# Both S5 runs in the projection phase, seven PSUM slots for the first projection, and the last gate by halves, in a hybrid trunk step

## The chip, the cores and the metric

The kernel runs on one core of a Trainium2 chip. The metric is the time of one execution on the device in microseconds; the median of three runs stands for the kernel. The engines have the names of the profile: PE multiplies matrices, PEld loads their stationary operand, DVE, ACT and POOL work on elements, and SP issues the DMA transfers.

## The reference

One layer of a streaming encoder works on 2080 tokens: 2048 of a prompt and 32 of a second group with states of its own. All projections have 1024 rows; `w_in` is worked as 22 tiles of 128 columns and eight more for beta and alpha; the hidden layer has 2816 columns.

```python
hn   = rmsnorm(h, norm_mix)
proj = hn @ w_in                                   # qkv | z | beta,alpha | u5 | cc
ya = gdn_mixer(qkv, z, ba, ...)                    # conv of 4, chunked delta rule, state per head
yb = s5_mixer(u5, ...)                             # diagonal complex scan over time, GLU
yc = conformer_conv(cc, ...)                       # GLU, causal conv of 31 taps, LayerNorm, swish
h  = h + concat([ya, yb, yc]) @ w_out
hf = rmsnorm(h, norm_ffn)
h  = h + (silu(hf @ w1) * (hf @ w3)) @ w2
h  = h + (p @ pe_w) * sigmoid(h @ pe_gate_w)
y  = rmsnorm(h, norm_final)
```

The results are y and the new states of the three mixers, all in float32. The delta rule and the S5 scan pass a state from one stretch of tokens to the next; the conformer reads 30 earlier columns.

## The kernel before

Activations lie with features on partitions and tokens as columns. The tokens are cut into four blocks: three of 512 columns, and a last of 544, which is worked through in two chunks of 272 since a PSUM slot holds 512. Each float32 product is made of three passes, high x high, high x low and low x high, where high is the rounded part of an operand and low the rest. `dense` issues the 3 x 8 matmuls of one output tile into a PSUM slot. `load_weight` loads a weight tile (128 x 1024, 512 KB) into one of three buffers, ACT makes its high part (L94) and, the first time, POOL the low part (L98; DVE for w3); the low part is kept in memory and only loaded afterwards (L93).

Phase A (`PhaseA.block`) normalises a block's input, makes its halves hh and hl, and projects it tile by tile; DVE or ACT evacuates each tile (qkv: raw at L615; the conformer's input: xc at L723), and results go to memory. Phase F (`PhaseF.block`) takes a block from w_out to the output: it loads the heads' result mixT into hb and splits it into fah and fal (`split`, L77, L1134 to L1136), multiplies by w_out (evacuation L1173, square sums L1163 to L1167), normalises, runs hidden tiles (L1196 to L1204) and w2 (L1218), splits hb once more, and for each of eight tiles m runs the pe and gate products (L1241 to L1243). Then come the sum of squares over all columns and the final norm: `rms_bcast` makes the factor for each column, hb is multiplied by it (three tiles on POOL, L1251, five on DVE, L1253), and stored (L1254).

The three mixers, called heads, are Python generators ("chains"). A chain is a sequence of steps; each yield ends one, and a yield of k waits for k turns. `dense` calls `G.step`, which advances every chain once per `G.stage` columns of dense matmuls (7168, in phase F's first block 9216), so that heads are written in between dense tiles. `G.flush(done)` advances the chains until done. The head work of one block is `conf_of(b)`, whose convolution is 62 DVE instructions with the name cacc (L824, L826), and `gdn_of(b)`, two groups of 256 tokens and, in the last block, one of 32. S5 runs twice, `s5_unit` u = 0 and 1, each for two blocks (`G.UB` = 2).

Before the change the first S5 run, beside conformer 0 and gdn 0, is advanced in phase A. All other heads are one chain, `later_heads`, in phase F: conformer 1, gdn 1, conformer 2, S5 run 1, gdn 2, conformer 3, gdn 3. Block b of phase F starts only once heads b are done (`G.flush`). In the order that results, the convolution of conformer 1 has been pulled into phase A's last block.

Within an engine, instructions run in the order in which they are written out after the Tile scheduler has placed them: the code gives each a priority class (`G.first`, `G.heads`, `G.later`), and the scheduler's own timeline picks among those that are ready. PSUM has eight banks: three slots pd (`G.psD`) for dense tiles, one pn for norms, and two each of pc and pm (`G.psM`) for heads. SP's queue holds nearly all transfers in one order.

Of the kernel before, what the change touches and what calls it, by code (L numbers as in the profile page):

```python
# [2 lines left out]

# [5 lines left out]
F32 = mybir.dt.float32  # L9
# [414 lines left out]
def s5_unit(G, A, u, wp, pspool):  # L424
# [14 lines left out]
    for jq in range(4):  # L439
# [15 lines left out]
        Gm = ld("G", [P, 2, 2, P], G.s5c["G"][:, js])  # L455
        Toep = ld("Toep", [P, 4, P], G.s5c["Toep"][:, jq * 4:jq * 4 + 4])

        yield 3

        w = [wp.tile([P, 2, NCT], F32, tag=f"w{i}", name=f"w{i}") for i in range(2)]  # L460
        tm = [wp.tile([P, 2, NCT], F32, tag=f"tm{i}", name=f"tm{i}") for i in range(4)]
# [50 lines left out]
                else:  # L512
                    V.tensor_copy(S1[half[h], js, i], X[h][half[i], :, NC])

        yield 4

        ys = wp.tile([P, 4, NCT], F32, tag="ys", name="ys")
        ysv = ys.rearrange("p (j h) c -> p j h c", h=2)
# [25 lines left out]
        nc.scalar.activation(t, t, AF.Tanh, scale=math.sqrt(2.0 / math.pi))  # L544
        nc.scalar.activation(yf, yf, AF.Copy, scale=0.25)
        V.scalar_tensor_tensor(gq[:, jh], t, 1.0, yf, op0=ALU.add, op1=ALU.mult)
        yield 1 if jh == 0 else 5
    spc = 512 // NCT
    for j in range(2):
        yb = wp.tile([P, n], F32, tag="yf", name="yb")  # L550
# [21 lines left out]
class PhaseA:  # L572


    def __init__(self, G, A, ctx):
        self.G, self.A = G, A
        nc = G.nc
        V = nc.vector
        E = lambda name, bufs=1, **k: ctx.enter_context(G.tc.tile_pool(name=name, bufs=bufs, side="left", reuse_waits="tile", **k))
        self.wp = E("aw", 2)  # L580
        self.xp = E("ax", 12)
        cp = E("ac")

# [49 lines left out]
    def block(self, b):  # L633
# [481 lines left out]
class PhaseF:  # L1115
# [22 lines left out]
    def block(self, b):  # L1138
# [19 lines left out]
            hb.append(h)  # L1158
        ssum = wp.tile([P, n], F32, tag="ssum", name="ssum2", bufs=1)

        def squares(m):
            if m == 0:
                nc.scalar.activation(ssum, hb[m], AF.Square)  # L1163
            else:
                sq = wp.tile([P, n], F32, tag="t0", name="sq2")
                nc.scalar.activation(sq, hb[m], AF.Square)
                V.tensor_tensor(ssum, ssum, sq, op=ALU.add)  # L1167

        for m in range(KD):
            w = load_weight(G, A.w_out[m], KD, "out", m)  # L1170
# [57 lines left out]
            self.split(x, y, mx, k % 2)  # L1228
            ph.append((x, y))
        ssum = wp.tile([P, n], F32, tag="ssum", name="ssum3", bufs=1)  # L1230
        for m in range(KD):
            if m % 4 == 0:
                wp4 = load_weight(G, A.pe_w[m:m + 4].rearrange("m p k c -> p m k c"), (4, 2), "pe", m)
            wpe = [x[:, m % 4] for x in wp4]
            wg = load_weight(G, A.pe_gate[m], KD, "gate", m)
            for c0, cn in ch:
                cs = slice(c0, c0 + cn)
                pe = dense(G, G.psD, "pd", wpe, lambda k: ph[k][0], lambda k: ph[k][1], [0, 1], c0, cn)
                pg = dense(G, G.psD, "pd", wg, lambda k: ah[k], lambda k: al[k], ks, c0, cn)
                th = wp.tile([P, 512], F32, tag="t1", name="gth2")[:, :cn]  # L1240
                nc.scalar.activation(th, pg[:, :cn], AF.Tanh, scale=0.5)  # L1241
                V.scalar_tensor_tensor(th, th, 1.0, pe[:, :cn], op0=ALU.add, op1=ALU.mult)
                V.scalar_tensor_tensor(hb[m][:, cs], th, 0.5, hb[m][:, cs], op0=ALU.mult, op1=ALU.add)  # L1243
            squares(m)
            if m < 3:
                nc.scalar.activation(hb[m], hb[m], AF.Copy, scale=self.g3[:, m:m + 1])
        bc = wp.tile([P, n], F32, tag="bc", name="bc3", bufs=1)
        rms_bcast(G, wp, G.psN, "pn", ssum, n, bc)
        for k in range(KD):
            if k < 3:  # L1250
                nc.gpsimd.tensor_tensor(hb[k], hb[k], bc, op=ALU.mult)  # L1251
            else:
                V.scalar_tensor_tensor(hb[k], hb[k], self.g3[:, k:k + 1], bc, op0=ALU.mult, op1=ALU.mult)  # L1253
            nc.sync.dma_start(A.yT[:, k, t0:t0 + n], hb[k])  # L1254


@with_exitstack
def trunk_kernel(ctx: ExitStack, tc: tile.TileContext, A):
# [8 lines left out]
    def at(which):  # L1267
# [121 lines left out]
    def conf_of(b):  # L1389
        with R(f"cc_{b}") as wp:  # L1390
            yield from conf(b, wp)

    def s5_of(u):
        with R(f"s5_{u}") as wp:
            yield from s5_unit(G, A, u, wp, G.psM)

    def gdn_of(b):
        with R(f"gd_{b}", 2) as sp:
            for i in range(2):
                state[0] = yield from gdn_part(b, i, state[0], sp)  # L1400

    def run(*gens):

        for g in gens:
            yield from g

    with ExitStack() as cx:
        pa = PhaseA(G, A, cx)
        pa.block(0)

        box = {}

        def first_s5():
            while "w5" not in box:
                yield 1
            yield from s5_unit(G, A, 0, box["w5"], G.psM)
            box["done"] = True

        def first_heads():
            with R("s5i") as tp:  # L1420
                yield from s5_init(G, A, tp, G.psM)
            with R("s5_0") as w5:
                box["w5"] = w5
                yield from conf_of(0)
                yield from gdn_of(0)
                while "done" not in box:
                    yield 1

        G.start(first_heads())
        for b in range(1, NB):  # L1430
            if b == G.UB:
                G.start(first_s5())
            pa.block(b)
        if NB == G.UB:
            G.start(first_s5())
        G.flush()
    pf = PhaseF(G, A, ctx)
    ready = [0]

    def later_heads():  # L1440
        for b in range(1, NB):
            yield from conf_of(b)
            if b % G.UB == 0:
                yield from s5_of(b // G.UB)
            yield from gdn_of(b)
            ready[0] = b

    G.start(later_heads())
    for b in range(NB):
        G.flush(lambda: ready[0] >= b)  # L1450
        G.stage = STAGE.get(b, STAGE["A"])
        pf.block(b)

# [114 lines left out]
```

## Time and profile before

| | |
|---|---|
| median of three runs | 2884.57 us (2880.83 to 2887.48) |
| the profiled execution | 2888.11 us, its span 2886.3 us |
| mean granted clock | 0.979 |
| bytes moved by DMA | 565.32 MB |
| ACT, POOL busy | 935.2 us (32%), 549.4 us (19%) |

The profile shows one execution. Its rows are of three kinds: the page (busy time of each engine, a strip of 40 slices), tables by stretch of time, and single instructions with what they waited for. A name such as `ps_d<-fah,wh_gate` reads output from inputs; ps_d is a dense tile, fah and fal are the halves of an activation, wh and wl those of a weight. The share of busy time is a mean over the stages, so that a stage with an idle PE is looked for by its stretch.

### The profile page before, as it was taken

How to read it: one execution, taken by the hardware profiler on the slowest of the kernel's cores; microseconds unless marked ns; L12 is line 12 of the kernel's file. 1: busy time of each engine (PE TensorE's matmuls, PEld its weight loads, DVE VectorE, ACT ScalarE, POOL GpSimd, SP SyncE). 2: the span in 40 equal slices, each digit the busy share in tenths (PEclk: the TensorE clock that was granted, in tenths of full speed). 3: DMA queues.
4: the chain of work that ended last, by engine and by line, in shares of the span. 5: the costliest groups of instructions: out<-in, count | busy, mean ns of one | idle time of the engine just before them, and what ended most of it. 6: DMA issues, size and time to landing. Idle time of an engine off the chain costs nothing.

```text
span 2886.3 us, 41015 instructions
## 1 busy us (share of the span) xinstructions
PE 2763.9 (96%) x15300; PEld 2359.9 (82%) x15300; DVE 1751.6 (61%) x3933; ACT 935.2 (32%) x1409; POOL 549.4 (19%) x460
## 2 busy tenths in 40 slices
PE   7899999999999999899999999999999979999997
PEld 5668778898878887688888887778888869999997
DVE  8969765865675847966563755856464733333343
ACT  4243423313422222343422333342332423222232
POOL 5731312234232323421010101000010110000000
PEclk9999999999999999999999999999999979999998
DMA  6578777657654555487665657566565654555553
GB/s 225 170 252 269 248 227 227 199 181 245 206 185 167 190 168 200 152 288 220 216 183 176 187 174 242 187 207 192 172 193 154 197 193 149 174 175 176 175 187 107
DMA packets 278919, 565.32 MB, mean 196 GB/s; under 512 B 67344, under 2 KB 126880, under 8 KB 278576
## 3 DMA queue, kind: packets, MB, share of 16 engines
q1 hardware_dynamic: 278720, 562.70, 60.4%
q8 instruction: 121, 1.98, 0.3%
q14 instruction: 78, 0.64, 0.1%
HBM read 457.76 MB, written 104.25 MB: 195 GB/s over the span
## 4 chain that ended last, share of the span: by engine, by line
PE 64%; DVE 8%; DMA 3%; issue 3%; SPq 1%; ACT 1%; POOL 0%; DVEq 0%; POOLq 0%; ACTq 0%
PE ps_d L122 57%; DVE cacc L826 3%; PE ps_kk L935 1%; PE ps_q L1013 1%; PE ps_z L1026 1%; DVE ct L982 1%; DVE cx L983 1%; DVE hb L1218 1%; DMA xd<-cx 1%; DMA hb<-mixT 1%; PE ps_vn L1069 0%; PE ps_o L1083 0%; PE ps_o L1084 0%; PE ps_s L1076 0%; PE ps_ks L1056 0%
## 5 line engine op out<-in xcount | busy, mean ns | idle before, releaser
L94 ACT ACTIVATE wh_w<-wr_w 128x1024 fp32r<-128x1024 f32 (+1 forms) x272 | 281.3, 1034 | 762.9 <-PE ps_d L122 551.4
L122 PE MATMUL ps_d<-fah,wh_w 128*128 128x512 f32 (+1 forms) x1760 | 379.4, 354 | 7.4 <-DVE fa L1196 2.9
L122 PE MATMUL ps_d<-fal,wh_w 128*128 128x512 f32 (+1 forms) x1760 | 376.5, 353 | 0.0
L122 PE MATMUL ps_d<-fah,wl_w 128*128 128x512 f32 (+1 forms) x1760 | 376.1, 353 | 0.0
L122 PEld LDWEIGHTS ps_d<-fah,wh_w 128*128 128x128 f32 x1760 | 291.1, 189 | 53.6 <-issue 4.0
L122 PEld LDWEIGHTS ps_d<-fal,wh_w 128*128 128x128 f32 x1760 | 291.4, 189 | 43.2
L122 PEld LDWEIGHTS ps_d<-fah,wl_w 128*128 128x128 f32 x1760 | 291.3, 189 | 43.2 <-issue 0.4
L1218 DVE TENSOR_TENSOR hb<-hb,ps_d 128x512 f32<-128x512 f32 (+1 forms) x240 | 139.7, 583 | 167.1 <-PE ps_d L122 166.7
L122 PE MATMUL ps_d<-acth,wh_w 128*128 128x512 f32 (+1 forms) x880 | 210.3, 355 | 9.1 <-DVE hb L1218 7.7
L122 PE MATMUL ps_d<-acth,wl_w 128*128 128x512 f32 (+1 forms) x880 | 210.1, 354 | 0.0
L122 PE MATMUL ps_d<-actl,wh_w 128*128 128x512 f32 (+1 forms) x880 | 208.6, 354 | 0.0
L826 DVE SCALAR_TENSOR_TENSOR cacc<-xc,cc_w,cacc 128x512 f32<-128x512 f32 (+1 forms) x240 | 189.4, 824 | 0.0
L122 PEld LDWEIGHTS ps_d<-acth,wh_w 128*128 128x128 f32 x880 | 148.6, 189 | 34.7 <-DVE hb L1218 6.1
L122 PEld LDWEIGHTS ps_d<-actl,wh_w 128*128 128x128 f32 x880 | 149.4, 189 | 22.2
L122 PEld LDWEIGHTS ps_d<-acth,wl_w 128*128 128x128 f32 x880 | 149.2, 189 | 22.2
L98 POOL TENSOR_TENSOR wl_w<-wr_w,wh_w 128x1024 fp32r<-128x1024 f32 (+1 forms) x46 | 108.2, 2351 | 253.9 <-ACT wh_w L94 226.3
L1201 DVE SCALAR_TENSOR_TENSOR fth<-ps_d,bc 128x512 f32<-128x512 f32 (+1 forms) x110 | 64.8, 589 | 132.0 <-PE ps_d L122 131.3
L1196 DVE TENSOR_TENSOR fa<-ps_d,bc 128x512 f32<-128x512 f32 (+1 forms) x110 | 64.5, 588 | 118.5 <-PE ps_d L122 109.4
L122 PE MATMUL ps_d<-hh,wh_qkv 128*128 128x512 f32 (+1 forms) x480 | 107.2, 365 | 13.8 <-DVE raw L615 13.0
L1204 DVE TENSOR_TENSOR actl<-fa,acth 128x512 fp32r<-128x512 f32 (+1 forms) x110 | 81.3, 739 | 51.3 <-ACT acth L1203 50.9
L1199 DVE SCALAR_TENSOR_TENSOR fa<-fth,fa 128x512 f32<-128x512 f32 (+1 forms) x110 | 73.1, 667 | 58.8 <-ACT fth L1198 58.6
L122 PE MATMUL ps_d<-hh,wl_qkv 128*128 128x512 f32 (+1 forms) x480 | 105.5, 361 | 2.3 <-POOL wl_qkv L98 2.3
(479 smaller groups left out, 4783.3 us busy)
## 6 DMA issues: line engine op xcount, KB each, us to landing
wr_w<-in_w SPq DMA_DIRECT2D x256, 512.0 KB, 4.3
wl_w<-lo_w SPq DMA_DIRECT2D x192, 512.0 KB, 4.0
lo_w<-wl_w SPq DMA_DIRECT2D x64, 512.0 KB, 2.9
wr_qkv<-in_w_in SPq DMA_DIRECT2D x48, 512.0 KB, 4.7
wl_qkv<-lo_qkv SPq DMA_DIRECT2D x36, 512.0 KB, 4.2
wr_out<-in_w_out SPq DMA_DIRECT2D x32, 512.0 KB, 5.2
wr_gate<-in_pe_gate SPq DMA_DIRECT2D x32, 512.0 KB, 4.3
wl_out<-lo_out SPq DMA_DIRECT2D x24, 512.0 KB, 5.9
```

The source lines that it names most:

```text
L94: nc.scalar.activation(wh, wr, AF.Copy)
L98: e.tensor_tensor(wl, wr, wh.bitcast(F32), op=ALU.subtract)
L122: nc.tensor.matmul(ps[:, :cn], a[:, i, :], x(k)[:, c0:c0 + cn], start=start and p_ == 0 and i == 0, stop=stop and p_ == 2 and i == K - 1)
L826: V.scalar_tensor_tensor(acc[:, j], xc[:, j, t:t + W], cn_.w[:, j, t:t + 1], acc[:, j], op0=ALU.mult, op1=ALU.add)
L935: nc.tensor.matmul(kk4[:, h - h0], kq[:, 2 * h, cw], kq[:, 2 * h:2 * h + 2, cw], start=True, stop=True)
L982: V.tensor_tensor(t, cx[:, 0:nq, j:j + 1].to_broadcast(sh), cu[:, j:j + 1, j + 1:].to_broadcast(sh), op=ALU.mult)
L983: V.tensor_tensor(cx[:, 0:nq, j + 1:], cx[:, 0:nq, j + 1:], t, op=ALU.subtract)
L1196: V.tensor_tensor(a, p1[:, :cn], bc[:, cs], op=ALU.mult)
L1199: V.scalar_tensor_tensor(a, th, 1.0, a, op0=ALU.add, op1=ALU.mult)
L1201: V.scalar_tensor_tensor(th, p3[:, :cn], 0.5, bc[:, cs], op0=ALU.mult, op1=ALU.mult)
L1204: V.tensor_tensor(fb[:, cs], a, fa[:, cs].bitcast(F32), op=ALU.subtract)
L1218: V.tensor_tensor(hb[m][:, c0:c0 + cn], hb[m][:, c0:c0 + cn], p_[:, :cn], op=ALU.add)
```

## The change

Three things are changed. First, both S5 runs are one chain of their own, `s5_chain`, started in phase A ahead of the third block; run u waits until the projections of its blocks have been written (`G.u5`). Its three long yields are shortened by one turn each. The other heads are `heads_chain`, in which conformer 1 follows as soon as both S5 runs are done; phase A's flush stops once heads 0 are done. One of twelve input buffers of phase A (pool "ax") goes. Second, in block 0's projection the dense tiles take turns on seven PSUM slots instead of three. Third, in the last block the pe and gate products, the square sums, the final norm and the stores are run for the first 272 columns, then for the second; the weights are loaded twice for it. In the second half all eight final products are on DVE, and the pre-scaling on ACT is left out.

```diff
 def dense(...):
     if ps is None:
+        pool, tag = next(G.banks) if G.banks else (pool, tag)
         ps = pool.tile([P, 512], F32, tag=tag, name="ps_d")
 # s5_unit
-        yield 3
+        yield 2
...
-        yield 4
+        yield 3
...
-        yield 1 if jh == 0 else 5
+        yield 1 if jh == 0 else 4
 # PhaseA
-        self.xp = E("ax", 12)
+        self.xp = E("ax", 11)
...
+        G.u5 = b + 1
 # PhaseF.block
-        for m in range(KD):
...
-            for c0, cn in ch:
...
-            squares(m)
-            if m < 3:
-                nc.scalar.activation(hb[m], hb[m], AF.Copy, scale=self.g3[:, m:m + 1])
-        rms_bcast(G, wp, G.psN, "pn", ssum, n, bc)
...
+        for grp in ([[c] for c in ch] if len(ch) > 1 else [ch]):
+            gs = slice(grp[0][0], grp[-1][0] + grp[-1][1])
+            end = b == G.NB - 1 and gs.stop == n
+            for m in range(KD):
+                if m % 4 == 0:
+                    wp4 = load_weight(G, A.pe_w[m:m + 4]..., (4, 2), "pe", m)
+                wg = load_weight(G, A.pe_gate[m], KD, "gate", m)
+                for c0, cn in grp:
...
+                squares(m, gs)
+                if m < 3 and not end:
+                    nc.scalar.activation(hb[m][:, gs], hb[m][:, gs], AF.Copy, scale=self.g3[:, m:m + 1])
+            rms_bcast(G, wp, G.psN, "pn", ssum[:, gs], gs.stop - gs.start, bc[:, gs])
+            for k in range(KD):
+                if k < 3 and not end:
+                    nc.gpsimd.tensor_tensor(hb[k][:, gs], hb[k][:, gs], bc[:, gs], op=ALU.mult)
+                else:
+                    V.scalar_tensor_tensor(hb[k][:, gs], hb[k][:, gs], self.g3[:, k:k + 1], bc[:, gs], op0=ALU.mult, op1=ALU.mult)
+                nc.sync.dma_start(A.yT[:, k, t0 + gs.start:t0 + gs.stop], hb[k][:, gs])
 # trunk_kernel
+    def s5_chain():
+        while "w5" not in box:
+            yield 1
+        for u in range(G.NU):
+            while G.u5 < (u + 1) * G.UB:
+                yield 1
+            yield from s5_unit(G, A, u, box["w5"], G.psM)
+            box["runs"] = u + 1
+    def ready(b):
+        return box["ready"] >= b and box["runs"] * G.UB > b
+    def heads_chain():
+        with R("s5i") as tp:
+            yield from s5_init(G, A, tp, G.psM)
+        with R("s5_0") as w5:
+            box["w5"] = w5
+            yield from conf_of(0)
+            yield from gdn_of(0)
+            box["ready"] = 0
+            while box["runs"] < G.NU:
+                yield 1
+        for b in range(1, NB):
+            yield from conf_of(b)
+            yield from gdn_of(b)
+            box["ready"] = b
...
+        G.banks = cycle([(G.psD, "pd"), (G.psM, "pc"), (G.psD, "pd"), (G.psM, "pm"), (G.psD, "pd"), (G.psM, "pc"), (G.psM, "pm")])
         pa.block(0)
+        G.banks = None
+        G.start(heads_chain())
         for b in range(1, NB):
-            if b == G.UB:
-                G.start(first_s5())
+            if b == min(G.UB, NB - 1):
+                G.start(s5_chain())
             pa.block(b)
-        G.flush()
+        G.flush(lambda: ready(0))
...
-    def later_heads():
-        for b in range(1, NB):
-            yield from conf_of(b)
-            if b % G.UB == 0:
-                yield from s5_of(b // G.UB)
-            yield from gdn_of(b)
-            ready[0] = b
```

The order of the instructions shows the effect at three places. On PE, at the passage from the third to the last block of phase F, before: the gate's last pass, then the last group of the delta rule (ps_vn to ps_ot) with the final norm of the third block (ps_ss, ps_bc) among it, then w_out.

```order
L122 MATMUL ps_d<-fal,wh_gate 128x512 x8
L1069 MATMUL ps_vn<-rk,X 32x128 x4
L151 MATMUL ps_ss<-ones,ssum_20261 128x1 x4
L1076 MATMUL ps_s<-vn,rk 128x128 x4
L1083 MATMUL ps_o<-Sd_18742,kq 32x128
L1084 MATMUL ps_o<-vn,AQ 32x128
```

```order
L134 MATMUL ps_bc<-ident,rso 128x128 x4
L1109 MATMUL ps_ot<-ident,o 128x32 x4
L122 MATMUL ps_d<-fah,wh_out 128x272 x22
```

Now, at the same place:

```order
L125 MATMUL ps_d<-fah,wh_gate 128x512 x8
L125 MATMUL ps_d<-fah,wl_gate 128x512 x8
L125 MATMUL ps_d<-fal,wh_gate 128x512 x8
L125 MATMUL ps_d<-fah,wh_out 128x272 x8
L125 MATMUL ps_d<-fah,wl_out 128x272 x8
L125 MATMUL ps_d<-fal,wh_out 128x272 x5
```

The last group of the delta rule has moved up; its last ps_ot stands 227 dense matmuls ahead of the third block's end.

SP's queue at that passage, before: the last group's transfers (xd, X, zy), the third block's stores, then mixT and its loads into hb.

```order
L991 DMA X<-xd 32x4x32
L88 DMA wr_out<-in_w_out 128x1024
L1105 DMA zy<-zgd_70 128x4x32
L1384 DMA out_gdn_s<-S 128x512
L1254 DMA out_yT<-hb 128x512 x8
L1111 DMA mixT_62<-zy 128x4x32
L1155 DMA hb<-mixT_62 128x544 x8
```

Now the loads of hb stand among the third block's gate weights:

```order
L89 DMA wr_pe<-in_pe_w 128x4x256
L1115 DMA mixT_62<-zy 128x4x32
L1159 DMA hb<-mixT_62 128x544 x3
L94 DMA wl_gate<-lo_gate2_11547 128x1024
L1159 DMA hb<-mixT_62 128x544 x5
L89 DMA wr_gate<-in_pe_gate 128x1024
```

They have moved ahead of the gate's last low parts (tiles 3 to 7) and of the stores.

On DVE, in the first block's w_out, before: evacuations of w_out (L1173) and square sums (L1167) alone.

```order
L1167 TENSOR_TENSOR ssum_6921<-ssum_6921,sq_7051 128x512
L1173 TENSOR_TENSOR hb<-hb,ps_d 128x512
L1167 TENSOR_TENSOR ssum_6921<-ssum_6921,sq_7092 128x512
L1173 TENSOR_TENSOR hb<-hb,ps_d 128x512
L1167 TENSOR_TENSOR ssum_6921<-ssum_6921,sq_7133 128x512
```

Now three or six steps of conformer 1's convolution stand between two evacuations:

```order
L1177 TENSOR_TENSOR hb<-hb,ps_d 128x512
L830 SCALAR_TENSOR_TENSOR cacc<-xc,cc_w,cacc 128x512 x3
L1171 TENSOR_TENSOR ssum_7449<-ssum_7449,sq_7625 128x512
L830 SCALAR_TENSOR_TENSOR cacc<-xc,cc_w,cacc 128x512 x3
L1177 TENSOR_TENSOR hb<-hb,ps_d 128x512
```

That convolution has moved here from the projection phase. On SP, in the last block's gate, the first half's stores now stand in the queue ahead of the second half's last weights:

```order
L89 DMA wr_gate_26299<-in_pe_gate 128x1024
L1262 DMA out_yT<-hb_20699 128x272
L1262 DMA out_yT<-hb_20684 128x272
```

```order
L1262 DMA out_yT<-hb_20719 128x272
L94 DMA wl_gate_26257<-lo_gate5_11754 128x1024
L94 DMA wl_gate_26302<-lo_gate6_11820 128x1024
L89 DMA wr_gate_26344<-in_pe_gate 128x1024
L94 DMA wl_gate_26347<-lo_gate7_11886 128x1024
```

Eight stores have moved in ahead of three low parts and one weight.

More of the change, by code (lines that the diff above doesn't have):

```diff
@@ L2 @@
 from contextlib import ExitStack, contextmanager
+from itertools import cycle
 import concourse.bass as bass
@@ L1159, in block, with squares @@
         ssum = wp.tile([P, n], F32, tag="ssum", name="ssum2", bufs=1)
-        def squares(m):
+        def squares(m, cs=slice(0, n)):
             if m == 0:
-                nc.scalar.activation(ssum, hb[m], AF.Square)
+                nc.scalar.activation(ssum[:, cs], hb[m][:, cs], AF.Square)
             else:
-                sq = wp.tile([P, n], F32, tag="t0", name="sq2")
-                nc.scalar.activation(sq, hb[m], AF.Square)
-                V.tensor_tensor(ssum, ssum, sq, op=ALU.add)
+                sq = wp.tile([P, n], F32, tag="t0", name="sq2")[:, cs]
+                nc.scalar.activation(sq, hb[m][:, cs], AF.Square)
+                V.tensor_tensor(ssum[:, cs], ssum[:, cs], sq, op=ALU.add)
         for m in range(KD):
@@ L1230, in block @@
         ssum = wp.tile([P, n], F32, tag="ssum", name="ssum3", bufs=1)
-        for m in range(KD):
[L1232 to L1235, printed above, removed]
-            for c0, cn in ch:
[L1237 to L1243, printed above, removed]
-            squares(m)
-            if m < 3:
-                nc.scalar.activation(hb[m], hb[m], AF.Copy, scale=self.g3[:, m:m + 1])
@@ L1247, in block @@
-        bc = wp.tile([P, n], F32, tag="bc", name="bc3", bufs=1)
-        rms_bcast(G, wp, G.psN, "pn", ssum, n, bc)
[L1249 to L1254, printed above, removed]
+        bc = wp.tile([P, n], F32, tag="bc", name="bc3", bufs=1)
+        for grp in ([[c] for c in ch] if len(ch) > 1 else [ch]):
[3 more added lines that the diff above has]
+                if m % 4 == 0:
+                    wp4 = load_weight(G, A.pe_w[m:m + 4].rearrange("m p k c -> p m k c"), (4, 2), "pe", m)
+                wpe = [x[:, m % 4] for x in wp4]
+                wg = load_weight(G, A.pe_gate[m], KD, "gate", m)
+                for c0, cn in grp:
+                    cs = slice(c0, c0 + cn)
+                    pe = dense(G, G.psD, "pd", wpe, lambda k: ph[k][0], lambda k: ph[k][1], [0, 1], c0, cn)
+                    pg = dense(G, G.psD, "pd", wg, lambda k: ah[k], lambda k: al[k], ks, c0, cn)
+                    th = wp.tile([P, 512], F32, tag="t1", name="gth2")[:, :cn]
+                    nc.scalar.activation(th, pg[:, :cn], AF.Tanh, scale=0.5)
+                    V.scalar_tensor_tensor(th, th, 1.0, pe[:, :cn], op0=ALU.add, op1=ALU.mult)
+                    V.scalar_tensor_tensor(hb[m][:, cs], th, 0.5, hb[m][:, cs], op0=ALU.mult, op1=ALU.add)
+                squares(m, gs)
[8 more added lines that the diff above has]
+                nc.sync.dma_start(A.yT[:, k, t0 + gs.start:t0 + gs.stop], hb[k][:, gs])
@@ L1277, in at @@
             tc.cur_priority = G.pr[old]
+    G.banks = None
     G.chains = []
+    G.u5 = 0
     G.acc = 0
@@ L1391, in conf_of @@
             yield from conf(b, wp)
-    def s5_of(u):
-        with R(f"s5_{u}") as wp:
-            yield from s5_unit(G, A, u, wp, G.psM)
     def gdn_of(b):
@@ L1405, in run @@
             yield from g
+    box = {"ready": -1, "runs": 0}
+    def s5_chain():
[22 more added lines that the diff above has]
+            box["ready"] = b
@@ L1407, in trunk_kernel @@
     with ExitStack() as cx:
         pa = PhaseA(G, A, cx)
+        G.banks = cycle([(G.psD, "pd"), (G.psM, "pc"), (G.psD, "pd"), (G.psM, "pm"), (G.psD, "pd"), (G.psM, "pc"), (G.psM, "pm")])
         pa.block(0)
[L1411 to L1427, printed above, removed]
@@ L1429, in trunk_kernel @@
-        G.start(first_heads())
+        G.banks = None
+        G.start(heads_chain())
         for b in range(1, NB):
-            if b == G.UB:
-                G.start(first_s5())
+            if b == min(G.UB, NB - 1):
+                G.start(s5_chain())
             pa.block(b)
-        if NB == G.UB:
-            G.start(first_s5())
-        G.flush()
+        if NB == 1:
+            G.start(s5_chain())
+        G.flush(lambda: ready(0))
     pf = PhaseF(G, A, ctx)
-    ready = [0]
-    def later_heads():
-        for b in range(1, NB):
-            yield from conf_of(b)
-            if b % G.UB == 0:
-                yield from s5_of(b // G.UB)
-            yield from gdn_of(b)
-            ready[0] = b
@@ L1448, in trunk_kernel @@
-    G.start(later_heads())
     for b in range(NB):
-        G.flush(lambda: ready[0] >= b)
+        G.flush(lambda: ready(b))
         G.stage = STAGE.get(b, STAGE["A"])
```

## The prediction

> **What bounds the kernel now.** I read the page's totals and slices first, then the stretches in which TensorE idles, the list of TensorE's waits, and the timeline at those places. In the page the first row gives busy time, share of the span and instructions of each engine; the others give busy tenths in 40 slices of 72 us, PEclk the granted clock.
>
> ```profile
> PE 2763.9 (96%) x15300; PEld 2359.9 (82%) x15300; DVE 1751.6 (61%) x3933; ACT 935.2 (32%) x1409; POOL 549.4 (19%) x460
> PE   7899999999999999899999999999999979999997
> DVE  8969765865675847966563755856464733333343
> PEclk9999999999999999999999999999999979999998
> ```
>
> PE is busy 96% of 2886.3 us, and the change takes no dense matmul away; only waits and lowered clock can be won. They sit in the first slices, slice 17, slice 33 and at the end. The windows below (from:to, length, busy us and instructions of PE, PEld, DVE, ACT, POOL, then clock, DMA share, GB/s) cover block 0's projection, the first w_out, two conformer stretches, the start of the last block, its hidden layer, and the tail.
>
> ```profile
> 62.00:155.00 93.00, 77.35 (x312) 61.69 (x310) 92.27 (x214) 25.85 (x37) 66.47 (x78) 0.91 0.54 178
> 706.00:772.00 66.00, 65.28 (x299) 53.38 (x298) 38.98 (x45) 27.19 (x37) 18.80 (x9) 1.00 0.66 225
> 1128.00:1212.00 84.00, 68.83 (x269) 51.66 (x268) 83.13 (x99) 25.15 (x37) 34.91 (x17) 0.94 0.45 156
> 1789.00:1860.00 71.00, 65.35 (x284) 52.66 (x284) 69.56 (x103) 23.98 (x32) 6.23 (x5) 0.98 0.65 224
> 2315.00:2360.00 45.00, 24.55 (x120) 18.78 (x119) 18.67 (x34) 10.59 (x16) 10.63 (x8) 0.62 0.55 189
> 2420.00:2805.00 385.00, 385.00 (x3072) 385.00 (x3072) 138.08 (x312) 105.68 (x161) 5.35 (x4) 1.00 0.54 175
> 2866.00:2886.30 20.30, 2.81 (x15) 2.09 (x15) 9.15 (x12) 1.76 (x4) 6.04 (x4) 0.60 0.29 110
> ```
>
> PE loses 15.7, 15.2, 5.7, 20.4 and 17.5 us in rows 1, 3, 4, 5 and 7, and more by the clock; the second row, the first w_out, loses 0.7, and the hidden layer nothing: there a matmul of 272 columns takes 385/3072 = 0.125. The waits (total, times, longest, us) name who was late:
>
> ```profile
> PE ps_d L122 <- DVE raw L615: 15.0, 7, 5.8
> PE ps_d L122 <- ACT fah L1134: 10.6, 7, 5.7
> PE ps_ot L1109 <- DVE o L1101: 10.1, 1, 10.1
> PE ps_d L122 <- DVE xc L723: 5.3, 1, 5.3
> PE ps_v L468 <- DMA c_PT<-s5PTre: 2.4, 1, 2.4
> PE ps_v L468 <- DMA c_PT<-s5PTim: 1.8, 1, 1.8
> ```
>
> **1. Start of the last block's w_out: −26.** S5's second run moves ahead, so heads 2 and 3 finish earlier; in the order the last head matmul now stands 227 dense matmuls (52 us at 0.23, by the rows behind) before the end of the preceding block. Timeline rows (start, us, instruction, idle before):
>
> ```profile
> 2313.52 2.00 PE L122 MATMUL ps_d<-fal,wh_gate 128*128 128x512 f32 x8
> 2319.97 1.47 PE L1069 MATMUL ps_vn<-rk,X 32*32 32x128 f32 x8 [4.45 <-DMA X<-xd]
> 2340.88 0.63 PE L1109 MATMUL ps_ot<-ident,o 32*128 32x32 f32 x4 [10.10 <-DVE o L1101]
> 2347.25 6.77 PE L122 MATMUL ps_d<-fah,wh_out 128*128 128x272 f32 x22 [5.74 <-ACT fah L1134]
> ```
>
> From the last gate matmul's end (2315.5) to the first w_out matmul 31.7 us pass, and 22 matmuls then take 6.77 instead of 2.76 (22 x 0.125): 35.7 lost. What stays: the head's and the norm's matmuls (24.55 busy in 2315:2360, of which 12.75 are w_out's from 2347.25 on: 11.8 at half clock, 6 at full); and some 3.5 for w_out's input, whose eight halves ACT makes after the gate has let go of the buffers. 35.7 − 9.5 = 26. Bounds: −30 if the halves come without delay (35.7 − 6), −20 if the head's matmuls keep their 11.8 in their new place. At the boundary before, ACT waits for the loads too:
>
> ```profile
> 1778.63 0.63 ACT L1134 ACTIVATE fah<-hb 128x512 fp32r<-128x512 f32 x1 [4.91 <-DMA hb<-mixT]
> 1772.32 2.00 PE L122 MATMUL ps_d<-fah,wl_gate 128*128 128x512 f32 x8
> 1774.16 2.00 PE L122 MATMUL ps_d<-fal,wh_gate 128*128 128x512 f32 x8
> 1779.32 0.50 PE L122 MATMUL ps_d<-fah,wh_out 128*128 128x512 f32 x1 [3.16 <-ACT fah L1134]
> 1780.59 6.11 PE L122 MATMUL ps_d<-fah,wh_out 128*128 128x512 f32 x17 [0.78 <-ACT fah L1134]
> ```
>
> Eight matmuls of 512 columns go in 1.84 (1772.32 to 1774.16), 0.23 each. This boundary loses 3.2 + 0.8 + 2.2 (6.11 against 17 x 0.23) = 6.1. Its last head now ends 352 matmuls, 81 us, earlier; the wait for the loads goes and that for the halves, 3.5, is late next: **−3** (0 to −6).
>
> **2. The conformers: +6.** Without S5 between them, the 62 DVE accumulations of conformer 1 move from the projection into the first w_out, those of 2 from the end of the first block's gate over the whole of it, those of 3 from the third block's w_out to the second block's hidden layer and gate.
>
> ```profile
> 225.00:294.00 69.00, 0.17 (x2) 0.28 (x2) 43.93 (x62) 1.00 0.78 252
> 1128.00:1212.00 84.00, 0.76 (x4) 0.56 (x4) 59.25 (x62) 0.94 0.45 156
> 1177.71 3.20 DVE L826 SCALAR_TENSOR_TENSOR cacc<-xc,cc_w,cacc 128x512 f32<-128x512 f32 x2
> 1173.14 4.05 DVE L826 SCALAR_TENSOR_TENSOR cacc<-xc,cc_w,cacc 128x512 f32<-128x512 f32 x6
> 1177.31 2.39 POOL L98 TENSOR_TENSOR wl_gate<-wr_gate,wh_gate 128x1024 fp32r<-128x1024 f32 x1 [9.04 <-ACT wh_gate L94]
> ```
>
> The first two rows are windows for the accumulations alone: 62 take 43.9 in the projection, 59.25 where POOL subtracts weights. Two beside a 2.39 us subtraction took 3.20, six without one 4.05: 1.9 is lost per subtraction. By the order, conformer 1 now runs from the third w_out tile to the sixth hidden tile, some 57 us of PE. DVE needs 43.9, then 15 for eight subtractions (706:772 has 9 POOL instructions in 66 us), then 20 of evacuations and sums (83.13 − 59.25 = 23.9 in 84 us of 1128:1212): 79 against 57. The excess is 22; six of it PE's three slots can cover, so **+16** (0 to 23), nearest to 1128:1212, where PE lost 15.2 in the same company. Conformer 2 cost 15.2 and 4 to 5 of clock there and now spreads over eight tiles, still beside subtractions: **−5** (−13 to +8). Conformer 3 cost 5.7 and 1.4 in 1789:1860; where it goes POOL rarely subtracts: **−5** (−7 to 0).
>
> Skill against row: the Trainium skill, "SBUF — State Buffer", section "SBUF: two separate sides", says the port pair of DVE and GpSimd is an exclusive lock, the loser blocked for the other's whole instruction. The 1.9 agrees nearly; with the full 2.39, eight subtractions would cost 19, not 15, and this term be +20. It speaks against the change.
>
> ```profile
> 1201.01 3.36 PE L122 MATMUL ps_d<-fah,wh_gate 128*128 128x512 f32 x7 [2.97 <-ACT gth L1241]
> 1200.00:1205.00 5.00, 3.99 (x11) 3.21 (x12) 5.00 (x5) 1.90 (x3) 2.55 (x1) 0.66 0.26 93
> ```
>
> Seven matmuls take 3.36 instead of 1.61 after 2.97 us of idleness, clock 0.66: such a stall costs 1.7 more than its length. The six covered microseconds may be eaten by this, which the upper bound holds. The Trainium skill, "TensorE: Matmul & The Clock Gate", section "HAM oscillation", puts the danger at gaps over about 3.4 us; this row's gap is shorter, the measurement decides.
>
> **3. S5's second run in the projection: +4.** It adds no PE work; its tables are loaded before it, and PE waited 2.4 + 1.8 for them in the first run. Those 4.2 I take again (0 to 9, twice that; no gain, since in the old place it showed no wait of its own). What DVE does for it lies beside dense work that has DVE to spare (38.98 of 66 in 706:772).
>
> **4. Seven slots in block 0: −9.** PE waited 15.0 for raw (evacuations of qkv) and 5.3 for xc: 20.3, with a clock of 0.91 beside it. More slots let PE run ahead, but DVE is busy 92.27 of 93 in 62:155 and its order hardly changes, so a wait returns when DVE's queue sets the end. Between 0 and −22 I take −9, nearer to zero because DVE is full.
>
> **5. Pool "ax" 12 to 11: +1.5.** One tile fewer for the projection's input; it hits the prefetch of the next block only. Nearest is one late split or load, 0 to 2.8.
>
> **6. Gate and norm of the last block by halves: +1.**
>
> ```profile
> 2868.91 1.25 PE L151 MATMUL ps_ss<-ones,ssum 128*128 128x1 f32 x10 [3.03 <-DVE ssum L1167]
> 2874.87 6.88 DVE L1253 SCALAR_TENSOR_TENSOR hb<-hb,g,bc 128x544 f32<-128x544 f32 x5 [2.66 <-ACT bc L139]
> 2866.34 0.44 DVE L1242 SCALAR_TENSOR_TENSOR gth<-gth,ps_d 128x272 f32<-128x272 f32 x1 [2.88 <-ACT gth L1241]
> 2805.00:2866.00 61.00, 60.39 (x479) 59.93 (x477) 19.32 (x39) 21.25 (x35) 0.12 (x1) 1.00 0.37 123
> 1240.00:1260.00 20.00, 20.00 (x105) 16.30 (x104) 12.42 (x24) 5.96 (x8) 5.71 (x4) 1.00 0.91 324
> ```
>
> Tail: the final scaling falls from 6.88 to eight at 0.44 (3.5): −3.4; squares, sums and broadcast over 272 columns, by halving their share, −1.8; shorter last store −0.5: −5.7. Against it: the first half's norm puts its own small matmuls on PE, 1.6, and its sum stands in the order between the second half's matmuls, so that a wait for ssum delays the gate behind it, 1.7 (3.03 in the row less what is queued ahead). Loads: 8 gate and 2 pe weights twice, high and low, are 20 more of 512 KB, 10.5 MB, and SP's queue has eight stores ahead of three of them. The 61 us of the gate moved 7.5 MB at 123 GB/s; with 10.5 and about 1.1 of stores it is 19.1 in 61 us, 313 GB/s. The row reaches 324 over 20 us, so it just fits: +3.5 (0, to 13 at the 259 of the next row).
>
> ```profile
> 165.00:345.00 180.00, 174.05 (x799) 134.53 (x799) 137.26 (x256) 77.16 (x117) 40.06 (x49) 0.97 0.80 259
> ```
>
> −5.7 + 1.6 + 1.7 + 3.5 = +1.
>
> **Sum:** −26 − 3 + 6 + 4 − 9 + 1.5 + 1 = −25.5. The profiled execution took 2888.1, so 2862.6 there; it stands 3.5 (0.12%) above the median 2884.57, which gives **2859**.
>
> **Rivals.**
> - *Slots idle.* DVE sets block 0's pace as before, and S5's loads cost double: −25.5 + 9 + 5, 2873. For it: 92.27 of 93. Against: waits of 5.8 at a time come in bursts, and bursts are what slots absorb.
> - *Conformer 1 hidden.* PE's slots and DVE's slack take it, as in the projection at 225, which lost next to nothing: −16 more, 2843. Against: POOL's subtractions.
> - *Slower: convolution exposed.* If DVE, being in order, puts the accumulations ahead of what w_out needs (19 in a row stand before the first hidden tile), PE idles for all of conformer 1: 59 instead of 16, 2902. It decides once conformer 1 costs 47 or more. For: DVE's 83.13 of 84 at 1128. Against: the order otherwise puts 3 to 6 between evacuations.
> - *Weights late in the halves.* At 259 GB/s 19.1 MB take 74 us, not 61: 9.5 over my 3.5, 2869. Slower than before would need 205 GB/s.
> - *The boundary stays.* The heads are early, but a load of mixT or the weights behind it come late through SP's one queue, and w_out still waits as long: 2859 + 26, 2885, no change. Against: the loads now stand among the gate's weights, ahead of those of its last tiles.
>
> **How the numbers follow.** A change under 0.2% (5.8 us) can't be told from none here. Forecast, 2850 to 2868: 0.47. Slots idle 0.15. Conformer hidden 0.15. Late weights 0.09. Boundary stays 0.05. Convolution exposed 0.06. The other 0.03 is divided over all signs: faster 0.87, same 0.06, slower 0.07. The range 2840 to 2880 takes in the first four cases, 0.86, and leaves out the rest and the outer spread of those, about 0.2.
>
> **What would show it.** After the last gate matmul of the third block, w_out within 6 us at full clock and no row o L1101 ahead of it; the w_out window of the first block with DVE full and PE losing about 16; the waits for raw about halved; a tail near 15 us; waits for wh_gate or wl_gate in the second half if loads are late. The prediction is wrong if conformer 1 costs nothing or over 40, or if the wait at the boundary only changes its name.

## The result: slower, and the profile after

The changed kernel takes 2911.15 us (median of four, 2908.99 to 2915.45) against 2885.98 in the same series: ratio 1.0092, 95% interval 1.0074 to 1.0111. Forecast was 2859, faster. The profiled execution took 2908.99 us, its span 2907.2, so 20.9 more than the span before.

The page after, same rows as those shown of before:

```profile
PE 2765.9 (95%) x15303; PEld 2357.5 (81%) x15303; DVE 1761.0 (61%) x3952; ACT 944.0 (32%) x1429; POOL 540.6 (19%) x461
```

```profile
PE   8789799999999999989999999999999999999997
DVE  8967874655887576697637449763745543333343
PEclk9899999999999999999999999999999999999999
```

PE's busy time is the same within 2 us; 18.9 us more of idleness make the difference. The dip at slice 33 is gone, and slices 2, 3 and 5 have become worse. A table by stages places it. First before, then after: the projection, then the four blocks of phase F, each from its first w_out matmul (from:to, length, PE busy, and so on; the third number from the end is the clock).

```profile
0.00:683.00 683.00, 634.55 (x3487) 528.59 (x3488) 508.78 (x1291) 226.55 (x359) 231.35 (x267) 0.97 0.69 220
683.00:1231.00 548.00, 528.06 (x2490) 429.36 (x2489) 377.85 (x626) 171.55 (x247) 189.85 (x95) 0.99 0.57 191
1231.00:1779.00 548.00, 543.84 (x2688) 448.07 (x2686) 317.69 (x768) 189.50 (x276) 59.88 (x46) 1.00 0.64 202
1779.00:2347.00 568.00, 539.64 (x2576) 439.42 (x2576) 354.81 (x840) 192.82 (x295) 51.58 (x41) 0.97 0.60 192
2347.00:2886.30 539.30, 517.82 (x4062) 514.44 (x4062) 192.43 (x410) 154.82 (x236) 16.69 (x12) 0.97 0.51 168
```

```profile
0.00:737.00 737.00, 661.41 (x3683) 548.51 (x3684) 510.07 (x1391) 238.51 (x377) 240.59 (x289) 0.96 0.69 218
737.00:1301.00 564.00, 531.87 (x2493) 432.75 (x2492) 413.56 (x663) 167.55 (x242) 189.75 (x89) 0.98 0.55 185
1301.00:1838.00 537.00, 525.48 (x2512) 430.89 (x2511) 334.92 (x711) 188.15 (x278) 47.35 (x38) 0.99 0.61 194
1838.00:2370.00 532.00, 529.65 (x2547) 432.20 (x2545) 298.94 (x751) 186.05 (x283) 42.31 (x32) 1.00 0.61 197
2370.00:2907.20 537.20, 517.51 (x4077) 513.17 (x4075) 203.53 (x440) 163.70 (x254) 20.63 (x17) 0.99 0.58 191
```

Length less PE busy is PE's idle time: 48.5, 19.9, 4.2, 28.4, 21.5 before; 75.6, 32.1, 11.5, 2.4, 19.7 after. The third block idles 26 less, and the other stages together lost 45. In the projection PE is also busy 27 us longer. Some 21 of these are the matmuls of S5's second run, which the second block of phase F no longer has (18 less there); most of the rest is lowered clock.

What block 0's projection waits for now (timeline of PE after; at the end of a row the idle time before it and its releaser):

```profile
93.89 3.78 PE L125 MATMUL ps_d<-hh,wl_qkv 128*128 128x512 f32 x8 [10.88 <-POOL wl_qkv L99]
...
119.60 3.78 PE L125 MATMUL ps_d<-hh,wh_qkv 128*128 128x512 f32 x8 [6.66 <-ACT wh_qkv L95]
```

```profile
PE ps_d L125 <- POOL wl_qkv L99: 13.4, 3, 10.9
PE ps_d L125 <- ACT wh_qkv L95: 7.6, 2, 6.7
PE ps_d L125 <- DVE raw L618: 4.8, 3, 3.4
```

The waits for raw (15.0 in all before) fell to 4.8, none of it in block 0, and in their place PE waits for the halves of the next weight, 13.4 for POOL and 7.6 for ACT (total, times, longest). Eight matmuls after the two long waits take 3.78 instead of 1.84: the clock has dropped. Conformer 1 in the first w_out, conformer 2 in the first gate, the boundary, and the tail:

```profile
764.00:842.00 78.00, 67.10 (x276) 53.41 (x275) 78.00 (x101) 22.53 (x30) 22.42 (x8) 0.91 0.40 143
1233.00:1301.00 68.00, 58.34 (x240) 45.26 (x239) 62.53 (x71) 23.08 (x34) 27.28 (x12) 0.97 0.61 218
2313.00:2370.00 57.00, 56.31 (x248) 45.44 (x246) 19.36 (x29) 24.81 (x36) 2.42 (x2) 1.00 0.69 240
2886.00:2907.20 21.20, 8.99 (x63) 8.06 (x63) 7.96 (x21) 3.54 (x8) 0.85 (x1) 0.76 0.21 76
```

DVE is busy all of 764 to 842, and PE loses 10.9 and a tenth of its clock there. Up to the first w_out matmul of the last block (2370) PE now idles only 0.7 us in 57.

### The profile page after: what moved, and what is told of

Same layout as the page of the kernel before. It is cut to its first block, busy times and chain, and to the rows that moved or that the text cites. A ratio compares the mean times of both kernels' runs of the same rounds, so it can differ in the third digit from the quotient of the medians.

```text
span 2907.2 us, 41101 instructions
## 1 busy us (share of the span) xinstructions
PE 2765.9 (95%) x15303; PEld 2357.5 (81%) x15303; DVE 1761.0 (61%) x3952; ACT 944.0 (32%) x1429; POOL 540.6 (19%) x461
## 4 chain that ended last, share of the span: by engine, by line
PE 68%; DVE 15%; DMA 8%; issue 4%; ACT 2%; POOL 1%; SPq 1%; DVEq 0%; POOLq 0%; ACTq 0%
PE ps_d L125 60%; DVE cacc L830 5%; DVE gacc L628 1%; PE ps_kk L939 1%; DMA xk<-in_xT 1%; DMA xc<-xcd 1%; DMA sild<-gacc 1%; PE ps_q L1017 1%; PE ps_z L1030 1%; DVE fal L1140 1%; DMA mixT<-zy 1%; PE ps_ks L1060 1%; PE ps_o L1087 1%; PE ps_o L1088 1%; PE ps_s L1080 0%
## 5 line engine op out<-in xcount | busy, mean ns | idle before, releaser
L125 PE MATMUL ps_d<-fah,wh_w 128*128 128x512 f32 (+1 forms) x1760 | 385.4, 358 | 15.5 <-DVE fa L1200 7.8
L830 DVE SCALAR_TENSOR_TENSOR cacc<-xc,cc_w,cacc 128x512 f32<-128x512 f32 (+1 forms) x240 | 203.2, 883 | 0.0
L125 PE MATMUL ps_d<-hh,wl_qkv 128*128 128x512 f32 (+1 forms) x480 | 106.6, 364 | 13.4 <-POOL wl_qkv L99 13.4
L1207 ACT ACTIVATE acth<-fa 128x512 fp32r<-128x512 f32 (+1 forms) x110 | 60.3, 548 | 141.6 <-DVE fa L1206 141.4
```

The costliest lines, as they stand in the source:

```text
L125: nc.tensor.matmul(ps[:, :cn], a[:, i, :], x(k)[:, c0:c0 + cn], start=start and p_ == 0 and i == 0, stop=stop and p_ == 2 and i == K - 1)
L830: V.scalar_tensor_tensor(acc[:, j], xc[:, j, t:t + W], cn_.w[:, j, t:t + 1], acc[:, j], op0=ALU.mult, op1=ALU.add)
L1207: nc.scalar.activation(fa[:, cs], a, AF.Copy)
```

## The experiments

Two theories stood at first. A: the seven slots are what costs, by what they do to the first blocks. B: the cost is in S5's move and the smaller input pool. Each part was built alone, from the kernel before. The ratios compare with executions of the kernel before in the same series, whose median was 2888.87 to 2890.61, while the first forecasts count from 2885; so it is the differences that compare with a forecast.

**Slots alone** (`e1_banks`).

```diff
+        G.banks = cycle([pd, pc, pd, pm, pd, pc, pm])   # as in the change
         pa.block(0)
+        G.banks = None
```

> The kernel before with seven PSUM slots in block 0's projection alone. Theory A (the slots are what costs: in the trace of the changed kernel the first two blocks lose 17 us by the third block's qkv, ahead of any work of S5's second run): 2885 + 15, near 2900. Theory B (the slots give nothing and cost nothing, the loss comes from S5's move and the smaller input pool): 2880 to 2887.

Measured: 2920.55 against 2890.61, ratio 1.0108 (1.0090 to 1.0127): theory A in kind and twice its size, as much as the whole change costs (the intervals overlap). Windows of this kernel: block 0 up to its z tiles, then to the third block's qkv, then the end of the projection from its last z tiles to w_out; behind them the same three stretches before.

```profile
0.00:148.00 148.00, 119.51 (x468) 91.27 (x469) 137.49 (x361) 49.56 (x74) 95.08 (x99) 0.92 0.60 194
148.00:391.00 243.00, 222.58 (x1002) 172.07 (x1001) 180.10 (x358) 97.79 (x150) 68.40 (x66) 0.94 0.75 241
657.00:718.00 61.00, 43.80 (x348) 40.42 (x347) 26.72 (x69) 16.05 (x31) 12.24 (x11) 0.86 0.40 130
```

```profile
0.00:155.00 155.00, 123.48 (x480) 94.94 (x480) 144.76 (x373) 54.37 (x81) 98.39 (x101) 0.91 0.60 198
155.00:380.00 225.00, 216.45 (x1002) 168.67 (x1003) 175.98 (x363) 93.05 (x145) 62.19 (x66) 0.98 0.78 251
656.00:683.00 27.00, 26.79 (x215) 26.36 (x214) 15.05 (x31) 7.77 (x16) 6.42 (x3) 1.00 0.59 183
```

Idle: 28.5 for 31.5 in block 0; 20.4 for 8.6 in the next stretch; 17.2 for 0.2 at the end. So the slots won 3 us of idleness where they are. In DVE's order four evacuations, scalar work and the conv products of block 1 now stand ahead of conformer 0's convolution (470 instructions ahead of its first step for 441); it begins at 250 us for 226, right behind an evacuation of block 1 at 249, and what follows it in the chain is late. That the new order is the reason is read from the rows; no run has seven slots with the old order. The heads of block 0 then end after the last projection matmul, where nothing covers them:

```profile
703.26 1.97 PE L1111 MATMUL ps_ot<-ident,o 128*128 128x128 f32 x8 [4.80 <-DVE o L1103]
706.02 2.30 PE L858 MATMUL ps_cf<-ident,ctk 128*128 128x128 f32 x8 [0.80 <-POOL ctk L855]
718.13 4.21 PE L124 MATMUL ps_d<-fah,wh_out 128*128 128x512 f32 x9 [9.80 <-ACT fah L1136]
```

**S5's move alone**, with its pool of 11 (`e2_s5`): the diff without `G.banks` and without the halves.

> S5's second run moved into the projection, with its shorter yields and the input pool of 11, without the seven slots and without the halves. Theory A: the boundary's gain of 26 and the loss beside the conformers and in the last projection block nearly cancel, 2885 to 2892. Theory B: all of the loss is here, 2905 to 2915.

Measured: 2902.58, ratio 1.0047 (1.0033 to 1.0062). Between the two theories, some 12 to 14 over the kernel before: the move neither breaks even nor holds all of the loss.

**Halves alone** (`e3_halves`): the diff in `PhaseF.block` only.

> The kernel before with the gate and final norm of the last block by halves alone. Both theories: the last block took 539.3 us in the kernel before and 537.2 in the changed one, so 2 us are won, 2881 to 2885; loads that come late would show as waits for wl_gate, 2.5 us in the changed kernel.

Measured: 2888.52, ratio 0.9993 (0.9982 to 1.0003), no change. After the last gate matmul 14.0 us pass for 20.4 before, as forecast, but the gate stage lost that and more (71.3 us for 61.3 in the profiled execution). It shows one wait of 3.1 for a low half of a weight, and half clock behind it, at 298 GB/s.

```profile
2860.45 2.18 PE L122 MATMUL ps_d<-fah,wl_gate 128*128 128x272 f32 x8 [3.09 <-DMA wl_gate<-lo_gate]
2801.00:2866.00 65.00, 60.03 (x443) 57.79 (x443) 23.90 (x52) 30.72 (x53) 4.31 (x5) 0.95 0.87 298
```

**The input pool alone** (`e4_ax11`): `E("ax", 12)` becomes `E("ax", 11)`.

> The kernel before with the projection's input pool of 11 tiles in place of 12, nothing else. Theory A: 2885 to 2888, as predicted (0 to 2.8). Theory B with the pool as the cause: block 1 waits for its halves, 2890 to 2902.

Measured: 2906.93, ratio 1.0062 (1.0048 to 1.0077), 16 us for one buffer of each half: the size of theory B, but not by its mechanism. The waits for the halves themselves hardly grew, from 9.5 to 11.7.

```profile
PE ps_d L668 <- ACT hh L77: 11.7, 7, 6.4
```

**Twelve high and eleven low halves** (`e8_hl11`): `bufs=11` on the tag "al" alone.

> The kernel before with 12 tiles for the high halves of the projection's input and 11 for the low ones. Theory A (PE waits for high halves that come late): 2888 to 2893. Theory B (one low half fewer made early is enough to put block 1's and the heads' instructions in another order): 2900 to 2908, as with 11 of both.

Measured: 2903.67, ratio 1.0055 (1.0037 to 1.0073): theory B. One low half less, made early, is enough. In both kernels DVE's order departs from that before at 41 us, in block 0; whether the late low half or the new order costs the 16 us stays open.

**S5's move and the halves, with 12 buffers** (`e5_s5h_ax12`). The diff is against the changed kernel.

```diff
-    glu_w = wp.tile([P, 2, 256], F32, tag="glu", name="glu")      # ahead of the loop in s5_unit
...
+    glu_w = wp.tile([P, 2, 256], F32, tag="ys", name="glu")       # behind it
-        self.xp = E("ax", 11)
+        self.xp = E("ax", 12)
-        G.banks = cycle([...])
```

> The changed kernel without the seven slots and with the input pool back at 12 (its room comes from loading S5's GLU weight late, into the buffer of ys). Theory A (the pool's 16 us is a cost of its own, which the move of S5 pays for the room its tiles take): 2890 + 12 - 16 - 2, 2884. Theory B (the pool's cost alone comes from the order that the planner happened to find, and doesn't subtract): 2897 to 2904, as the S5 move with 11.

Measured: 2895.63, ratio 1.0026 (1.0014 to 1.0039): neither figure. Against `e2_s5` (1.0047) the larger pool brings some 6, not 16. DVE's order is that of before up to 219 us, so the move can be read more cleanly here. Its stages:

```profile
0.00:721.00 721.00, 659.20 (x3679) 550.45 (x3680) 506.26 (x1390) 237.39 (x373) 237.35 (x287) 0.96 0.70 223
721.00:1284.00 563.00, 534.65 (x2494) 435.02 (x2495) 413.35 (x672) 171.39 (x245) 191.69 (x90) 0.98 0.55 184
1284.00:1826.00 542.00, 531.09 (x2512) 432.66 (x2511) 328.14 (x703) 187.33 (x278) 48.44 (x38) 0.99 0.61 192
1826.00:2358.00 532.00, 529.59 (x2548) 432.33 (x2547) 300.18 (x751) 186.88 (x283) 42.53 (x32) 1.00 0.62 197
```

Idle: 61.8, 28.4, 10.9, 2.4 against 48.5, 19.9, 4.2, 28.4 before. The 26 that the third block wins are paid back as 13 + 8 + 7.

**Slots on top of that** (`e7_s5h_ax12_banks`): the same with `G.banks`.

> As the run with S5 moved, halves and pool of 12, with the seven slots in block 0 again. Theory A (of the 30 us that the slots cost alone, about 17 are heads that end after the last projection and are exposed there, which S5's own chain with its early flush avoids; the rest, later convolution and waits in block 1, stays): 12 to 15 more than that run. Theory B (the slots cost 30 wherever they are): 30 more. Theory C (they win once the heads are early): less than that run.

Measured: 2912.32, ratio 1.0075 (1.0053 to 1.0096), some 14 over the run without (1.0075 − 1.0026): theory A. Without the end of the projection at stake, the loss beside block 1 remains; the same stretch with the slots (first row) and without (second, `e5_s5h_ax12`):

```profile
148.00:388.00 240.00, 219.28 (x1017) 171.18 (x1017) 181.00 (x363) 97.14 (x150) 63.96 (x65) 0.96 0.76 246
155.00:381.00 226.00, 219.36 (x1019) 172.00 (x1020) 177.21 (x376) 93.65 (x145) 69.85 (x67) 0.97 0.79 255
```

Since this kernel is the whole change but for the pool and the place of the GLU weight, and the change had 1.0092, the pool is worth some 5 us there; the intervals overlap.

**Conformer 1 back in the projection** (`e6_s5h_ax12_conf1`). The diff is against the run with S5 moved, halves and pool of 12.

```diff
             box["ready"] = 0
+            if NB > 1:
+                yield from conf_of(1)
             while box["runs"] < G.NU:
                 yield 1
         for b in range(1, NB):
-            yield from conf_of(b)
+            if b > 1:
+                yield from conf_of(b)
```

> As the run with S5 moved, halves and pool of 12, but conformer 1 is written ahead of the wait for S5's runs, so that it lies in the projection again. Theory A (conformer 1 costs what the first phase F block lost, 561 us for 548, beside POOL's subtractions): 13 less than that run. Theory B (DVE is needed there by S5, and the loss moves to the projection's last block): within 4 of that run.

Measured: 2916.63, ratio 1.0096 (1.0077 to 1.0115): 20 more than without, against both theories. From the last z tiles to w_out 81 us pass (40 in `e5_s5h_ax12`). PE idles 22.7 us in one piece behind the convolution; S5's second run ends at 766 us, after conformer 1, and phase F begins only then.

**Conformer 1 without its taps** (`e10_s5_without_conf1`): `range(1, 2 if b == 1 else TAPS)`.

> The S5 move with halves and pool of 12, in which conformer 1 leaves out 29 of its 31 taps (58 DVE instructions), a part of the computation. Theory A (conformer 1 beside POOL's subtractions is most of the 15 us by which the first phase F block grew): 11 to 16 less than the run with all taps, 2880 to 2885. Theory B (the growth is S5's rest and the norm's own waits): 0 to 5 less.

Measured: 2880.06, ratio 0.9967 (0.9954 to 0.9979), 16 less than `e5_s5h_ax12`. That is the size of theory A, but by luck: the first block, where it was expected, became 5 us longer, the second and third 15 and 6 shorter. The same 130 us from w_out on, with conformer 1 (first row, `e5_s5h_ax12`) and without (second, this run), then where conformers 2 and 3 came to lie in this run:

```profile
721.00:851.00 130.00, 117.82 (x495) 93.87 (x496) 114.24 (x147) 46.66 (x68) 45.21 (x22) 0.94 0.53 179
```

```profile
720.00:850.00 130.00, 129.56 (x577) 104.99 (x578) 101.64 (x177) 52.12 (x75) 55.16 (x29) 0.98 0.63 211
1149.00:1223.00 74.00, 60.72 (x242) 47.45 (x240) 74.00 (x84) 18.43 (x25) 30.30 (x14) 0.93 0.47 157
1661.00:1720.00 59.00, 59.00 (x258) 48.09 (x257) 59.00 (x87) 16.10 (x18) 0.00 (x0) 1.00 0.66 202
```

In its own stretch conformer 1 cost 11.7 of idleness and 4 points of clock over 130 us. Conformer 2 moved up into the end of w2, beside POOL, and PE idled 13.3 there, so the first block did not get shorter. Conformer 3 moved into the second block's hidden layer with w2 on either side, where POOL does nothing: DVE is full for 59 us, and PE loses nothing.

**The boundary by another way** (`e9_small_group_early`). S5 stays in its place. The group of the delta rule that stands at the boundary has a state of its own and needs nothing of the other groups; it becomes a chain beside conformer 3.

```diff
+    def small_group():
+        while "sp" not in dbox:
+            yield 1
+        Sd = sp.tile(...)                       # state in its own pool
+        Sd = yield from gdn_group(G, A, sp, G.psM, G.td_, 0, TS, 1, Sd, NB - 1, BLK, sp)
...
     def conf_of(b):
         with R(f"cc_{b}") as wp:
+            if b == min(3, NB - 1):
+                with R("gd_small", 2) as sp:    # opened here, the chain starts
```

> The kernel before, S5 in its old place and three slots, with the halves, and one more edit: the last group of the delta rule (32 tokens, a state of its own), which stands alone between the third block's last gate matmul and the last block's w_out, runs beside conformer 3, in a chain and a pool of its own. Theory A (the boundary's 35.7 us are won whenever the heads end early, and the move of S5 lost because of what it put into the projection and into the first two blocks): 2889 - 26 - 2 and some 2 back beside conformer 3, 2860 to 2866. Theory B (what is won at the boundary comes back at another wait): 2880 to 2890.

Measured: 2860.55 against 2889.31, ratio 0.9904 (0.9890 to 0.9918): theory A. At the boundary w_out follows the gate:

```profile
2321.04 2.00 PE L122 MATMUL ps_d<-fal,wh_gate 128*128 128x512 f32 x8
2322.88 1.13 PE L122 MATMUL ps_d<-fah,wh_out 128*128 128x272 f32 x7
2324.17 0.39 PE L122 MATMUL ps_d<-fah,wh_out 128*128 128x272 f32 x1 [0.16 <-ACT fah L1134]
```

**The same beside conformer 2** (`e11_small_group_conf2`): `min(2, NB - 1)`.

> As the run with the small group beside conformer 3, but beside conformer 2, in the first block's gate, where DVE was busy 83 of 84 us. Theory A: the boundary is won as well, but DVE's extra work there is exposed, 5 to 15 more than that run. Theory B (the group's work is small): the same within 4.

Measured: 2889.21, ratio 0.9998 (0.9987 to 1.0009): 29 over the run beside conformer 3, more than either theory. The wait now stands at the boundary before that one, since heads 2 end late:

```profile
1809.66 1.97 PE L1109 MATMUL ps_ot<-ident,o 128*128 128x128 f32 x8 [8.79 <-DVE o L1101]
1823.89 2.50 PE L122 MATMUL ps_d<-fah,wh_out 128*128 128x512 f32 x5 [12.27 <-ACT fah L1134]
```

**The small group alone, without the halves** (`e12_small_group_only`).

> The kernel before with the small group of the delta rule beside conformer 3 alone, without the halves: the boundary's share by itself. Theory A (boundary and halves add): 2 more than with the halves, 2862 to 2866. Theory B (the halves' shorter tail shows only once the boundary's half clock is gone, or the reverse): 2868 or more.

Measured: 2857.60 against 2889.01, ratio 0.9895 (0.9875 to 0.9914). It is some 31 us less, better than both theories, and the halves add nothing (the intervals of the two runs overlap). This one edit beats the kernel before by 1.05%, and so the slower changed kernel too.

## Why the prediction was wrong, point by point

**Step 1, the boundary (−26 and −3): right, somewhat small.** The third block shrank by 36 with S5's move, and the next one no longer starts at half clock. That its idleness fell by just 26 is coincidence: some 20 of these stood at the boundary (45 less 24.55 in 2315:2360) and 5.7 beside conformer 3. The boundary by itself is worth some 31 (`e12_small_group_only`); the 3.5 us reserved for w_out's halves did not appear (0.16 in the row above). At the boundary before it the wait went as well.

**Step 4, the slots (−9): the step that failed by its sign.** It is +30 alone, +14 in the company of S5's move. The premise was right, that DVE is full in block 0, and it was then used only to shorten the gain. I bounded the term by 0 on the bad side, with the argument that DVE's order hardly changes. In `e1_banks` it departs from that before at 30 us, and behind block 0 four of block 1's evacuations and their work pass ahead of conformer 0. Within block 0 the wait changed its name, from raw to the weight's halves, as the rival "slots idle" had it; that rival too priced it at nothing. The sign that I had named, fewer waits for raw, came true, and it did not show the loss.

**Step 3, S5 in the projection (+4): too small.** In the run with 12 buffers the projection grew by 38. By the starts of PE's rows, 21 of these are S5's matmuls, which the second block of phase F loses (23). The other 17 are cost: 13.4 of idleness, the rest clock. S5's waits for loads make 11.2 in that run (c_PT, Toep, and two behind xcd and sild), 7 more than before, within the bound of 9; a wait of 3.2 for w_out's halves at the end of the projection and one of 2.9 for the input of its last block make up most of what is left. That the old place "showed no wait of its own" was true, and was no price for the new one.

**Step 2, the conformers (+6): single convolutions came near, the sum was far too small.** In `e5_s5h_ax12` the first block of phase F is 15 us longer, and the second 17 once S5's 23 are taken off. Conformer 1 came near its size in its own stretch: 11.7 idle and some 5 of clock against 16. Where conformers 2 and 3 stand, PE idles 12.4 of 78 us at clock 0.98 (15.2 of 84 at 0.94 before) and 4.1 of 69 at full clock (5.7 of 71 at 0.98 before), so both gains exist. What the sum had at nothing is the start of the second block, in which conformer 2 ends (first two rows `e5_s5h_ax12`, then before; last, conformer 3 in `e5_s5h_ax12`):

```profile
1284.00:1345.00 61.00, 57.16 (x246) 43.57 (x245) 45.47 (x82) 31.88 (x53) 14.67 (x12) 0.97 0.77 262
1345.00:1400.00 55.00, 52.07 (x235) 42.90 (x235) 36.77 (x93) 18.04 (x23) 10.05 (x7) 0.94 0.49 144
1231.00:1292.00 61.00, 60.27 (x300) 49.64 (x299) 40.85 (x89) 23.16 (x34) 12.61 (x11) 1.00 0.84 281
1292.00:1347.00 55.00, 54.74 (x294) 45.30 (x294) 38.99 (x107) 19.82 (x26) 12.93 (x11) 1.00 0.73 226
1717.00:1786.00 69.00, 64.86 (x276) 50.90 (x275) 68.71 (x97) 21.87 (x30) 5.63 (x4) 1.00 0.60 189
```

PE idles 6.8 there for 1.0, with some 5 of clock besides; it waits for halves of the activations and for the norm's factor. The lack of S5's matmuls between them is not enough to cause it: in `e10_s5_without_conf1`, where conformer 2 ends in the first block, the second has no S5 run either, idles 2.4 and takes 526, which is 548 less 23. What delays those halves and the norm behind conformer 2 stays open.

**Step 5, the pool (+1.5): too small where it stands alone** (16), some 5 in the full change. There the waits for hh are 17.5, for 12.9 in `e7_s5h_ax12_banks` with 12 buffers. The bound of 2.8 priced one late tile; alone, the wait for it rose by 2.2 only, and the rest of the 16 lies elsewhere.

**Step 6, the halves (+1): right in its parts.** From `e12_small_group_only` to `e9_small_group_early` the gate grows from 61.3 to 67.4 us and the tail falls from 20.7 to 14.2, against +6.8 and −5.7 in the sum; the whole is within the measurement of none.

Both sums: −25.5 forecast; +7.5 (S5 and halves with 12 buffers), +14 (slots) and some 5 for the pool make the measured +25 (by the medians) to +27 (by the ratio). Conformer 1's accumulations alone, in the changed kernel:

```profile
764.00:842.00 78.00, 0.38 (x2) 0.28 (x2) 54.83 (x62) 0.91 0.40 143
```

The 62 take 54.83 beside eight POOL instructions, seven of them subtractions of weights, instead of 43.93 in 225:294 before, where POOL only copies small tiles: 1.4 more for each of the eight. The Trainium skill, "SBUF — State Buffer", section "SBUF: two separate sides", lets the loser wait for the whole instruction (2.4 and more here); the trace agrees in kind and shows less; why was not tried. The Trainium skill, "TensorE: Matmul & The Clock Gate", section "HAM oscillation", puts the danger to the clock at gaps over some 3.4 us; in `e3_halves` it fell behind one of 3.1, so here too the measurement decides.

## What to carry to other kernels

When work is moved off a boundary, price the place it goes to with rows of that place, not with the absence of waits in the old one: a block's convolution went with 0 to 15 us of idle PE by where it lay. Before moving the long piece, look for the piece that stands at the boundary itself and depends on nothing near it. Here a wait on a slot whose drain is full was not won by more slots, and the order behind it paid.

## What was not expected of the hardware

In `e10_s5_without_conf1` PE kept full speed through 59 us in which DVE was busy without a break and POOL idle; a full DVE alone need not be a loss. Beside POOL, with another block's 62 instructions, PE lost 13.3 of 74 us and the clock fell to 0.93. The two stretches differ in their place as well (hidden layer, and the end of w2 with its evacuations), so the share of POOL is not separated. And 298 GB/s over 65 us was sustained, yet one load still came 3.1 us late.
